# A delta-net layer on one Trainium2 core: v turned by DMA, merges in three pieces, half of an out-projection cut by depth, and a planner with other costs and another order

## The chip, the cores and the metric

The kernel runs on one core of a Trainium2 chip. Its engines are TensorE (PE, with its weight loads shown as PEld), VectorE (DVE), ScalarE (ACT), GpSimd (POOL) and SyncE (SP), whose queue issues nearly all the DMAs of the part in question. The metric is the device time of one execution in microseconds; lower is better. Only the times of the chip count.

## What is computed

A trunk of two layers over a sequence of 1024 rows of 1024 numbers, in float32. Layer 0 is a gated delta-net layer with a convolutional FFN behind it, layer 1 a chunked attention with another FFN. The change lies in the delta-net layer alone, whose reference is, cut to what matters:

```python
proj = xn @ w_in                                   # q, k, v, z and the gates
qkv = silu(causal_dwconv(proj[..., :A_CONV_WIDTH], conv_w))
q, k = l2norm(q) * 128 ** -0.5, l2norm(k)          # 8 heads of 128; v as it is
m = strict_lower(k_beta @ k.T * decay)             # per chunk of 64 rows
u, w = solve(m + eye, [v * beta, k_beta * exp(gcum)])
...
v_new = u_c - w_c @ state                          # chunk after chunk
o_c = qd @ state + a_c @ v_new
state = state * dec + ke.T @ v_new
...
o = rmsnorm(o, out_norm_w) * silu(z)
return o.reshape(bsz, seq, A_V_WIDTH) @ w_out      # + the residual stream
```

## The kernel before, in words

**The dense work.** A product of float32 matrices is done as three matmuls in a reduced format (L118, L119, L120: high part by high part, low by high, high by low), each 128x128 weights against 512 columns. Those three for one depth tile of 128 are called a unit here. A weight tile comes as `wraw` (SP), ACT rounds it to `whi`, and POOL subtracts four pieces to get `wlo` (L101 to L103).

**The delta-net stage.** 24 projection tiles (k, q and v of 8 heads, in the order of the list `ORDER`, L1329), each of two halves of 512 rows (s = 0, 1) and 8 units a half. Behind each half `project` (L601) runs the convolution and silu: `post` on ACT, `taps` on DVE, `silu` on ACT and POOL. A half of v is stored to `d_v` in float32; k and q go on in SBUF or by `d_kq`. Between the units stand the small products of the recurrence: `gram` (L672, `pg`) makes the 128x128 blocks `mn` per head, POOL's copies `cm` of their diagonal blocks go to `d_m`; `invert_blocks` (L785) inverts these on DVE and stores them by ACT's `W` to `d_u`; `merge` (L824), eight times, loads the inverses as `D` from `d_u` (two loads, one for each of its two heads) and joins blocks of 16 to 32, 64 and 128 rows in one PSUM tile `pm`, with copies on ACT (`X`, `TY`, `U`) and DVE (`U`) between its pieces; its last two pieces are eight 64x64 products each (L881 and L886). `prep` (L738) turns k (`pk`, four transposes on PE, scaled by ACT to `ke`), makes `pqk`, and loads a half of v as `vv` from `d_v`, turns it by four PE transposes into PSUM (`pv`, L778) and multiplies it by the scale `sk` on DVE (L780). `chain` and `output` (L912, L897) are the recurrence proper: `pc<-S,kq`, DVE's `vv`, `pc<-vv,U`, ACT's `y`, `pc<-y,ke`, DVE's `S`, and `pu` for the output. `finish` normalizes, `yz` and `split_yt` (L1039, L1056) multiply by the gate and split the result into `xh` (an ACT cast, L1057) and `xl` for the out-projection.

**The out-projection.** `out_tile(m, s)` (L1285): for each of 8 column tiles m of a half s, all 8 depth tiles in one PSUM tile, then one DVE addition of the residual, which a DMA brings as two u16 planes `xm` and POOL and DVE weave into `xs` (L1299). After each tile one step of the FFN's norm follows (`norm_steps`: ACT's square, and ACT's and POOL's `xh`, `xl` with h). All 8 tiles of s = 0 go first, then those of s = 1.

**What sets the order.** `Flow` (L198) is a list planner that runs while the program is built. It keeps a time `wv.T` for PE (0.69 us for a unit, `wv.pe(n, cost)` for small products) and times for ACT, DVE and POOL to which the code books costs (`wv.on("A", 0.8)`). A step goes in when those booked times say that its operands are ready, less a slack. The order of PE, ACT and DVE so made is kept by the compiler; the orders of SP and POOL are set by the framework's scheduler. Nothing of the booked numbers runs on the chip.

Of the kernel before, what the change touches and what calls it, by code (L numbers as in the profile page):

```python
# [16 lines left out]
P = 128  # L17
# [11 lines left out]
def trunk_kernel(  # L29
# [168 lines left out]
    class Flow(Weave):  # L198
# [4 lines left out]
        def __init__(self):  # L203
# [4 lines left out]
            self.brief, self.early, self.split_at, self.hold, self.far = False, 8, 8, None, 4.0  # L208

# [11 lines left out]
        def pe(self, n, dt=0.22):  # L221
            self.T += n * dt

# [46 lines left out]
        def _dense(self):  # L270
# [19 lines left out]
            self.T += 0.69  # L290
# [215 lines left out]
    d_v = [[dram.tile([P, HALF], F32, name=f"d_v{k}_{s}") for s in range(2)] for k in range(KT)]  # L506
    d_kq = [[dram.tile([P, HALF], F32, name=f"d_kq{k}_{j}") for j in range(2)] for k in range(KT)]
    with ExitStack() as ph:
        wp = ph.enter_context(tc.tile_pool(name="wp0", bufs=2, **SB))
        dp = ph.enter_context(tc.tile_pool(name="dp", bufs=1, **SB))  # L510
        tri = dp.tile([P, P], F32, name="tri")
# [12 lines left out]
        ba = dp.tile([P, 8, 16], F32, name="ba")  # L524
# [5 lines left out]
        eg, neg_eg, ekd, dec = gt("eg"), gt("neg_eg"), gt("ekd"), gt("dec")  # L530
        gc = dp.tile([P, 2, 8, 8], F32, name="gc")
        gcum, gtot = gc[:, 0], gc[:, 1]
        gr = dp.tile([64, P], F32, name="gr")
# [15 lines left out]
        ssk, ssq, sk, ck, nck = gt("ssk"), gt("ssq"), gt("sk"), gt("ck"), gt("nck")  # L549
# [3 lines left out]
        tiles = [0, 0]  # L553

# [19 lines left out]
        def split_tile(raw):  # L574
            wt = split_w(raw, [P, KT, P])
            wv.on("G", 2.75, wv.on("A", 1.0))
            return wt
# [23 lines left out]
        def project(m, dsts, key, store=None, n_from=0):  # L601
# [4 lines left out]
            def post(s, ps):  # L606
# [7 lines left out]
                def taps():  # L614
# [6 lines left out]
                    wv.later(wv.on("D", 2.19), silu)  # L621

                def silu():
# [8 lines left out]
                    wv.mark((key[0], key[1], s), t)  # L632

# [16 lines left out]
        def qnorm(hd, s):  # L650
# [5 lines left out]
            wv.pe(4, 0.11)  # L656
# [3 lines left out]
            slot[0] = wv.on("A", 1.9)  # L660
# [11 lines left out]
        def gram(t):  # L672
# [24 lines left out]
            for i, hd in enumerate(hds):  # L697
# [15 lines left out]
                wv.pe(4)  # L713
# [18 lines left out]
                wv.mark(("gram", hd, s), wv.on("G", 1.2, t_) + 2.5)  # L732
# [3 lines left out]
            wv.mark(("scale", t), wv.on("D", 3.5))  # L736

        def prep(hd, s):  # L738
# [12 lines left out]
            wv.pe(4, 0.11)  # L751
# [3 lines left out]
            slot[0] = wv.on("A", 1.4)  # L755
# [4 lines left out]
            vv = dp.tile([P, 4, P], F32, name="vv", tag="vv", bufs=4)  # L760
            nc.sync.dma_start(out=vv.rearrange("p c t -> p (c t)"), in_=d_v[hd][s])
# [6 lines left out]
            wv.pe(4)  # L768
# [4 lines left out]
            t = max(t, wv.on("G", 1.4))  # L773
# [5 lines left out]
            wv.pe(4, 0.11)  # L779
# [1944 lines left out]
```

## Time and profile before

| | |
|---|---|
| median of 3 runs | 2499.27 us (2497.41 to 2501.43) |
| span of the profiled execution | 2493.3 us |
| median less span | 6.0 us |
| PE busy | 2466.1 us, 99% of the span |
| DVE, POOL, ACT busy | 1842.5, 1523.0, 1442.1 us |
| granted TensorE clock | 9 tenths or more in all 40 slices |

The profile gives no time of its own for the profiled execution beside its span; the 6.0 us is what the median of the runs has over that span. A row of the profile gives an engine, a line of the kernel, an operation, "out<-in" by tile names, a shape, a count, and busy time or mean duration. A PE row's duration is longer than the distance to the next row, since matmuls are pipelined; what PE's stream costs is read from the starts. The delta-net stage with its out-projection runs from 21 us to 643 us, where the first matmul of the FFN stands.

### The profile page before, as it was taken

What the parts mean: (1) busy time and instruction counts of PE and PEld (TensorE: products, weight loads), DVE (VectorE), ACT (ScalarE), POOL (GpSimd) and SP (SyncE); (2) the same over time, 40 slices, a digit from 0 to 9 for tenths busy, and PEclk for the clock granted to TensorE, in tenths of its full rate; (3) what the DMA queues carried; (4) which work ended last, traced back from release to release, by engine and by line L of the source; (5) the groups of instructions that cost most, each with busy time, mean ns of one, the idle gap of its engine ahead of it and who ended that gap; (6) DMA issues with size and microseconds to landing.
All of it is one profiled execution on the core that took longest, in us unless ns stands there. A gap on an engine that the chain in (4) does not pass through costs nothing.

```text
span 2493.3 us, 39279 instructions
## 1 busy us (share of the span) xinstructions
PE 2466.1 (99%) x13785; PEld 2057.0 (83%) x13785; DVE 1842.5 (74%) x2985; ACT 1442.1 (58%) x2770; POOL 1523.0 (61%) x1548
## 2 busy tenths in 40 slices
PE   8999999999999999999999999999999999999998
PEld 6888888888888888888788888888877888888877
DVE  5665874567798888888866656666589788888886
ACT  6444546474465556565555666667456565666555
POOL 3655653357357777777626454455554777778774
PEclk9999999999999999999999999999999999999999
DMA  8734435565347777777841232333444799777788
GB/s 228 188 105 118 142 110 153 156 194 163 96 108 148 150 153 151 153 144 156 183 151 55 67 80 77 81 76 95 145 114 119 184 176 180 166 169 171 152 187 224
DMA packets 383877, 353.19 MB, mean 142 GB/s; under 512 B 97600, under 2 KB 304448, under 8 KB 383680
## 3 DMA queue, kind: packets, MB, share of 16 engines
q1 hardware_dynamic: 350704, 243.46, 34.4%
q0 software_dynamic: 28224, 98.58, 22.5%
q10 hardware_dynamic: 4752, 8.65, 0.9%
q8 instruction: 108, 1.77, 0.3%
q14 instruction: 89, 0.73, 0.1%
HBM read 182.25 MB, written 156.30 MB: 136 GB/s over the span
## 4 chain that ended last, share of the span: by engine, by line
PE 81%; POOL 6%; DVE 4%; issue 4%; DMA 2%; ACT 2%; SPq 0%; ACTq 0%; POOLq 0%; DVEq 0%
PE acc L118 8%; PE pu L1448 8%; PE acc L119 8%; PE acc L120 8%; PE pu L1446 8%; PE pu L1447 8%; PE pd L1448 3%; PE pd L1446 3%; PE pd L1447 3%; POOL ul L1412 3%; PE acco L118 2%; PE acco L120 2%; PE acco L119 2%; PE ptp L2353 2%; PE poT L2399 1%
## 5 line engine op out<-in xcount | busy, mean ns | idle before, releaser
L1412 POOL TENSOR_TENSOR ul<-r,uh 128x512 fp32r<-128x512 f32 x266 | 430.4, 1638 | 258.3 <-ACT uh L1434 253.5
L118 PE MATMUL acc<-xh,whi 128*128 128x512 f32 x896 | 369.3, 413 | 0.5 <-ACT xh L1094 0.5
L119 PE MATMUL acc<-xl,whi 128*128 128x512 f32 x896 | 352.1, 393 | 0.4 <-POOL xl L381 0.3
L120 PE MATMUL acc<-xh,wlo 128*128 128x512 f32 x896 | 351.3, 392 | 0.0
L103 POOL TENSOR_TENSOR wlo<-wraw,whi 128x256 fp32r<-128x256 f32 (+1 forms) x326 | 237.0, 758 | 107.8 <-ACT whi L101 105.3
L1434 ACT CAST uh<-r 128x512 fp32r<-128x512 f32 x289 | 177.1, 623 | 183.3 <-DVE r L1412 148.8
L1448 PE MATMUL pu<-xh,ul 128*128 128x512 f32 x524 | 204.4, 390 | 0.7 <-POOL ul L1412 0.7
L1446 PE MATMUL pu<-xh,uh 128*128 128x512 f32 x524 | 204.4, 390 | 0.7 <-ACT keep L1575 0.7
L1802 ACT COPY stage<-pd 128x1024 f32<-128x1024 f32 x180 | 175.3, 1014 | 49.7 <-PE pd L1448 48.8
L1447 PE MATMUL pu<-xl,uh 128*128 128x512 f32 x524 | 203.9, 389 | 0.0
L120 PEld LDWEIGHTS acc<-xh,wlo 128*128 128x128 f32 x896 | 168.5, 188 | 37.1
L2308 POOL TENSOR_SCALAR sS<-sS,st 128x640 f32<-128x640 f32 (+4 forms) x128 | 87.6, 691 | 178.4 <-DVE st L2306 168.2
L119 PEld LDWEIGHTS acc<-xl,whi 128*128 128x128 f32 x896 | 169.3, 189 | 28.4 <-POOL xl L381 2.5
L118 PEld LDWEIGHTS acc<-xh,whi 128*128 128x128 f32 x896 | 169.1, 189 | 27.5 <-ACT xh L1094 0.9
L1412 POOL TENSOR_TENSOR dl<-a,dh 128x512 fp32r<-128x512 f32 x90 | 153.3, 1703 | 47.4 <-ACT dh L1434 37.2
L1541 DVE SCALAR_TENSOR_TENSOR gate<-gpre,colt,gate 128x1023 f32<-128x1023 f32 (+2 forms) x92 | 176.5, 1919 | 2.5 <-ACT gate L1538 1.8
L1541 DVE SCALAR_TENSOR_TENSOR val<-vpre,colt,val 128x1023 f32<-128x1023 f32 x88 | 149.2, 1696 | 29.3 <-ACT val L1538 29.3
L2298 DVE CUSTOM_DVE_ANT_0 sS<-sc,bt 128x640 f32<-128x640 f32 (+4 forms) x128 | 84.1, 657 | 111.4 <-PE sc L2294 75.9
L1412 DVE TENSOR_TENSOR r<-r,r 128x512 f32<-128x512 f32 x160 | 130.3, 814 | 32.8 <-POOL ul L1412 31.7
L1412 DVE TENSOR_TENSOR el<-val,eh 128x512 fp32r<-128x512 f32 x90 | 85.4, 949 | 43.2 <-ACT eh L1434 43.2
L1448 PEld LDWEIGHTS pu<-xh,ul 128*128 128x128 f32 x524 | 98.4, 188 | 22.8 <-POOL ul L1412 1.4
L1446 PEld LDWEIGHTS pu<-xh,uh 128*128 128x128 f32 x524 | 98.4, 188 | 21.1 <-ACT keep L1575 1.1
(428 smaller groups left out, 7197.9 us busy)
## 6 DMA issues: line engine op xcount, KB each, us to landing
r<-in_f_w_up_dram SPq DMA_DIRECT2D x176, 256.0 KB, 4.5
d_r<-stage POOLq DMA_DIRECT2D x78, 512.0 KB, 8.1
d_c<-stage POOLq DMA_DIRECT2D x70, 512.0 KB, 8.4
a<-in_f_w_down_dram SPq DMA_DIRECT2D x72, 256.0 KB, 2.9
wraw<-in_a_w_in_dram SPq DMA_DIRECT2D x32, 512.0 KB, 4.5
d_e<-stage POOLq DMA_DIRECT2D x32, 512.0 KB, 8.3
wraw<-in_a_w_out_dram SPq DMA_DIRECT2D x16, 512.0 KB, 4.1
d_r<-h ACTq DMA_DIRECT2D x32, 256.0 KB, 2.8
```

The costliest lines, as they stand in the source:

```text
L103: nc.gpsimd.tensor_tensor(lo[:, c], raw[:, c], hi[:, c].bitcast(F32), op=ALU.subtract)
L118: mm(ps, hi[:, kw, wcol : wcol + P], rh[k][s], start=st, stop=False)
L119: mm(ps, hi[:, kw, wcol : wcol + P], rl[k][s], start=False, stop=False)
L120: mm(ps, lo[:, kw, wcol : wcol + P], rh[k][s], start=False, stop=sp)
L1412: tt = lambda eng, o, a, b, op: eng.tensor_tensor(o, a, b, op=op)
L1434: copy(hi, src)
L1446: mm(ps, w[0][:, cw], x[0], start=first, stop=False, skip_group_check=True)
L1447: mm(ps, w[0][:, cw], x[1], start=False, stop=False, skip_group_check=True)
L1448: mm(ps, w[1][:, cw], x[0], start=False, stop=last, skip_group_check=True)
L1541: nc.vector.scalar_tensor_tensor(t_[:, a:c1], p_[:, a - step : c1 - step], w[:, 2 - step : 3 - step], t_[:, a:c1], op0=ALU.mult, op1=ALU.add)
L1802: nc.scalar.copy(t_, ps)
L2308: nc.gpsimd.tensor_scalar(S, S, st[:, 3:4], 1.0, op0=ALU.mult, op1=ALU.mult)
```

## The change

Four things are changed in the delta-net layer; the FFNs and the attention are the same but for numbers in names.

1. **v.** After silu an ACT copy `cast` takes v apart into its two u16 halves (`th`), SP stores them to `d_v`, now 1024 rows of 128 u16, and `prep` loads them back by a DMA transpose as `vh`. ACT copies one plane into `vv`, POOL the other, and DVE multiplies by `sk` from SBUF. The four PE transposes `pv` and their PSUM tile go, for 16 halves.
2. **Merges.** The two last pieces of eight 64x64 products become three: four `low`; four pairs of `corner` and `low`; four `corner`. ACT's copies between them are halved in size, four instead of two.
3. **Out-projection, second half.** `out_deep` takes two column tiles at a time and depth tiles 0 to 3 for all 8 column tiles first, then 4 to 7: `h = ps + xs`, then `h = ps + h`. The number of matmuls is the same.
4. **The planner.** Booked costs and slack get other numbers, and `ORDER` is another. Some small tiles share buffers.

The diff, cut to its core:

```diff
-            self.T += 0.69
+            self.T += self.unit + self.mixed
...
-    d_v = [[dram.tile([P, HALF], F32, ...
+    d_v = [[dram.tile([SEQ, P], mybir.dt.uint16, ...
...
+                    if key[0] == "v":
+                        wv.later(t - 0.6, lambda: cast(th))
+                        return
...
+                def cast(th):
+                    nc.scalar.copy(planes(th), woven(d))
+                    nc.sync.dma_start(out=store[s].rearrange("(h b c) t -> c h b t", h=2, b=4), in_=th...)
...
-            vv = dp.tile([P, 4, P], F32, name="vv", tag="vv", bufs=4)
-            nc.sync.dma_start(out=vv.rearrange("p c t -> p (c t)"), in_=d_v[hd][s])
+            vh = dq.tile([P, 2, HALF], U16, name="vh", tag="vh")
+            nc.sync.dma_start(out=vh.rearrange("p h t -> p (h t)"), in_=d_v[hd][s], transpose=True)
...
-            slot = yield from wv.bank()
-            pv = paux.tile([P, HALF], F32, name="pv", tag="pa")
-            for c in range(4):
-                nc.tensor.transpose(pv[:, cs(c)], vv[:, c], ident)
-            wv.pe(4, 0.11)
-            nc.vector.tensor_tensor(vv, pv..., sk..., op=ALU.mult)
+            vv = dp.tile([P, 4, P], F32, name="vv", tag="vv", bufs=4)
+            w_ = woven(vv.rearrange("p c t -> p (c t)"))
+            nc.scalar.copy(w_[:, 0], vh[:, 0])
+            nc.gpsimd.tensor_copy(w_[:, 1], vh[:, 1])
+            yield max(wv.on("A", 0.78), wv.on("G", 0.93)) - wv.slack
+            nc.vector.tensor_tensor(vv, vv, sk..., op=ALU.mult)
...
-            for a, c, n in blocks:
-                mm(pm[64:128, n], mn[a][0:64, c, 64:128], TY[0:64, n], start=True, stop=True)
-            nc.scalar.copy(TY[64:128], pm[64:128])
-            yield wv.on("A", 0.6)
-            for a, c, n in blocks:
-                mm(pm[0:64, n], TY[64:128, n], U[64:128, n, 64:128], start=True, stop=True)
-            nc.scalar.copy(U[0:64, :, 64:128], pm[0:64])
+            for c in range(4):
+                low(0, c)
+            nc.scalar.copy(TY[64:128, 0:4], pm[64:128, 0:4])
+            yield wv.on("A", 0.4)
+            for c in range(4):
+                corner(0, c)
+                low(1, c)
+            nc.scalar.copy(TY[64:128, 4:8], pm[64:128, 4:8])
+            t_ = wv.on("A", 0.4)
+            close(0)
+            yield t_
+            for c in range(4):
+                corner(1, c)
+            close(1)
...
+        def out_deep(ms, k0):
+            raw = wp.tile([P, 4, 2 * P], F32, name="wraw", tag="wraw", bufs=2)
...
+            xms = [out_x(m, 1) for m in ms if k0 == 0]
...
-        ORDER = "k2 k0 k1 k3 q2 q0 q1 k5 k4 q3 v0 v1 k6 v2 v3 k7 q4 q5 q6 q7 v5 v4 v6 v7"
+        ORDER = "k2 k0 q0 q2 q1 k5 k4 k3 k1 k6 v1 v0 k7 q3 v2 v3 q4 q5 v5 v4 q6 q7 v6 v7"
-        wv.slack = 0.5
+        wv.slack = 0.6
+        wv.unit, wv.turnover = 0.683, 0.09
```

Three places show how the order moves. The first is SP's queue at the first merge of the program, before and after. `D` is the merge's load of the inverted blocks, `d_m` gram's store of a later head's blocks, `d_kq` a store of k or q.

```order
L630 DMA d_kq_0_154<-u 128x512
L808 DMA d_u_226<-W 128x512
L571 DMA wraw<-in_a_w_in_dram 128x8x128
L831 DMA D<-d_u_226 128x4x32 x2
L630 DMA d_kq_0_152<-u 128x512
L690 DMA d_e_0_204<-E 128x512
```

```order
L822 DMA d_u_224<-W 128x512
L577 DMA wraw<-in_a_w_in_dram 128x8x128
L845 DMA D<-d_u_224 128x4x32
L639 DMA d_kq_0_158<-u 128x512
L744 DMA d_m_221<-cm 128x4x32
L845 DMA D<-d_u_224 128x4x32
L759 DMA eq<-d_eg 128x4x128
L704 DMA d_e_0_207<-E 128x512
```

The two `D` loads stood together; now the second stands behind a `d_kq` and a `d_m` store.

The second is ACT's queue at the last merge, before and after. `X`, `TY` are the merge's copies, `ke` is of `prep`, `xh` are the casts of out-projection operands, `y` is of the chain.

```order
L865 COPY X<-pm 32x256 x2
L868 COPY TY<-T 32x8x32 x2
L1057 CAST xh_0_6133<-spare 128x512
L906 COPY vv<-pu 128x128
L876 COPY TY<-pm 32x8x32
L935 ACTIVATE y<-pc,ck 128x128 x2
L906 COPY vv<-pu 128x128
L883 COPY TY<-pm 64x512
```

```order
L879 COPY X<-pm 32x256 x2
L882 COPY TY<-T 32x8x32 x2
L768 ACTIVATE ke<-pk,ekd 128x128 x4
L1086 CAST xh_0_6294<-spare 128x512
L1086 CAST xh_0_6296<-spare 128x512
L1086 CAST xh_0_6298<-spare 128x512
L1086 CAST xh_0_6300<-spare 128x512
L1086 CAST xh_0_6302<-spare 128x512
L1086 CAST xh_0_6304<-spare 128x512
L964 ACTIVATE y<-pc,ck 128x128
L890 COPY TY<-pm 32x8x32
L935 COPY vv<-pu 128x128
```

One cast stood between the merge's first `TY` copies and its next; now six casts and four `ke` stand there.

The third is POOL's queue in the second half of the out-projection, at its first weight tiles; `xl` with `h` is of the FFN's norm.

```order
L1299 COPY xs<-xm 128x512
L103 TENSOR_TENSOR wlo<-wraw,whi 128x256 x4
L1299 COPY xs<-xm 128x512
L381 TENSOR_TENSOR xl_0_7200<-h_1_6584,xh_0_7199 128x512
L103 TENSOR_TENSOR wlo<-wraw,whi 128x256 x4
L1299 COPY xs<-xm 128x512
L381 TENSOR_TENSOR xl_0_7204<-h_3_6586,xh_0_7203 128x512
L103 TENSOR_TENSOR wlo<-wraw,whi 128x256 x4
```

```order
L103 TENSOR_TENSOR wlo<-wraw,whi 128x256 x4
L1328 COPY xs<-xm 128x512 x2
L103 TENSOR_TENSOR wlo<-wraw,whi 128x256 x4
L1328 COPY xs<-xm 128x512
L384 TENSOR_TENSOR xl_0_7225<-h_1_6599,xh_0_7224 128x512
L1328 COPY xs<-xm 128x512
L384 TENSOR_TENSOR xl_0_7229<-h_3_6601,xh_0_7228 128x512
L103 TENSOR_TENSOR wlo<-wraw,whi 128x256 x4
L1328 COPY xs<-xm 128x512 x2
L384 TENSOR_TENSOR xl_0_7233<-h_5_6603,xh_0_7232 128x512
```

A weight tile's `wlo` had one `xs` beside it; in the first depth half it has two.

## Rows read from the trace of the kernel before

**Rows 1.** The page's head, the program's one execution:

```profile
span 2493.3 us, 39279 instructions
```

**Rows 2.** Windows: length; PE, PEld, DVE, ACT, POOL busy; clock, DMA, GB/s:

```profile
21.00:643.00 622.00, 621.57 (x5019) 522.00 (x5018) 394.00 (x1013) 327.65 (x876) 340.69 (x448) 1.00 0.53 151
```

**Rows 3.** Timeline of PE, 172 to 174 us (start, us, line, tile, shape):

```profile
172.56 0.39 PE L120 MATMUL acc<-xh,wlo 128*128 128x512 f32 x1
172.78 0.60 PE L778 MATMUL pv<-ident,vv 128*128 128x128 f32 x4
...
173.69 0.40 PE L120 MATMUL acc<-xh,wlo 128*128 128x512 f32 x1
```

**Rows 4.** Timeline of PE, a 64x64 merge piece (two records a product):

```profile
187.87 0.38 PE L939 MATMUL pc<-y,ke 128*128 128x128 f32 x2
188.19 1.14 PE L881 MATMUL pm<-TY,mn 64*64 64x64 f32 x16
189.26 0.49 PE L903 MATMUL pu<-S,kq 128*128 128x128 f32 x2
```

**Rows 5.** Timeline of PE, a merge piece of 32x32 tiles:

```profile
152.28 0.75 PE L845 MATMUL pm<-T,mn 32*32 32x32 f32 x64
```

**Rows 6.** DMA issues: operation, count, KB each, median us from issue to landing:

```profile
D<-d_u SPq DMA_DIRECT2D x16, 64.0 KB, 3.3
```

**Rows 7.** One tile of the attention layer, vt (ns: least, median, most):

```profile
L2229 ACT COPY vt<-acc x14: 1012/1012/1012, 1377.3 to 1717.6; 128x1024 uint16<-128x1024 uint16 x14
```

**Rows 8.** One tile of the attention layer, vu, loaded by DMA transpose:

```profile
L2212 ACT COPY vf<-vu x28: 755/779/796, 1391.7 to 1740.2; 128x512 uint16<-128x512 uint16 x28
L2206 SPq DMA_TRANSPOSE vu<-d_vt x14: 1160/1171/2198, 1380.9 to 1730.7; - x14
```

**Rows 9.** One tile, xs, a half's worth of u16:

```profile
L1299 POOL COPY xs<-xm x16: 758/926/1242, 541.1 to 634.5; 128x512 uint16<-128x512 uint16 x16
```

**Rows 10.** One line, L1280, the input's DMA transposes at 11 to 73 us:

```profile
L1280 SPq DMA_TRANSPOSE xm<-in_x_dram x16: 1159/1258/6186, 11.4 to 72.6; - x16
...
DMA to landing us min/median/max: 3.1/3.8/7.8
```

**Rows 11.** Lines of ACT, 100 to 560 us (count, busy, mean ns, idle before):

```profile
L101 ACT CAST whi<-wraw 128x1024 fp32r<-128x1024 f32 x29 | 30.3, 1044 | 0.0
...
L689 ACT ACTIVATE E<-E,ngc 128x128 f32<-128x128 f32 x51 | 16.2, 391 | 0.3 <-DVE E L686 0.2
...
L610 ACT ACTIVATE u<-acc,colt 128x509 f32<-128x509 f32 x18 | 12.4, 686 | 29.7 <-PE acc L120 24.8 <-POOL u L627 2.6 <-issue 2.3
...
L806 ACT ACTIVATE W<-B,even 128x256 f32<-128x256 f32 x4 | 2.0, 506 | 2.8 <-DVE B L803 2.8
```

**Rows 12.** Lines of POOL, the same stretch:

```profile
L627 POOL TENSOR_TENSOR u<-u,th 128x512 f32<-128x512 f32 x27 | 35.2, 1305 | 2.2
L626 POOL TENSOR_SCALAR th<-th 128x512 f32<-128x512 f32 x38 | 24.5, 644 | 70.1 <-ACT th L625 50.9 <-DVE B L803 4.9 <-DVE u L616 4.8
...
L729 POOL COPY cm<-mn 32x128 f32<-32x128 f32 x52 | 16.7, 322 | 24.5 <-DVE mn L724 22.6
```

**Rows 13.** Lines of DVE, the same stretch:

```profile
L841 DVE STREAM_TRANSPOSE T<-D 128x256 f32<-128x256 f32 x8 | 3.5, 436 | 4.4 <-DMA D<-d_u 4.4
```

**Rows 14.** Timeline of ACT, 514 to 533 us:

```profile
515.02 2.18 ACT L1057 CAST xh<-spare 128x512 fp32r<-128x512 f32 x4
...
529.54 1.14 ACT L754 ACTIVATE ke<-pk,ekd 128x128 f32<-128x128 f32 x4
...
531.21 0.74 ACT L865 COPY X<-pm 32x256 f32<-32x256 f32 x2
```

**Rows 15.** Waits, 21 to 643 us (total us, times, longest):

```profile
DVE U L878 <- ACT TY L876: 12.6, 6, 3.8
```

**Rows 16.** Timeline of POOL, 607 to 624 us:

```profile
608.85 2.84 POOL L103 TENSOR_TENSOR wlo<-wraw,whi 128x256 fp32r<-128x256 f32 x4
...
613.37 1.30 POOL L381 TENSOR_TENSOR xl<-h,xh 128x512 fp32r<-128x512 f32 x1 [0.74 <-ACT xh L393]
```

More of the change, by code (lines that the diff above doesn't have):

```diff
@@ L1299, in out_tile, with out_end @@
                 (nc.gpsimd, nc.vector)[i].tensor_copy(hm[:, :, i], xm[:, i])
-            wv.on("G", 0.60), wv.on("D", 0.6)
-            for k in range(KT):
-                dense(ps, wt, 0, *acts, FULL[k : k + 1], s, first=k == 0, last=k == KT - 1)
-                if k < KT - 1:
-                    yield
+            wv.on("G", 0.95), wv.on("D", 0.69)
+            return ps, xs
+        def out_end(m, s, ps, xs):
             nc.vector.tensor_tensor(h[m][:, hs(s)], ps, xs, op=ALU.add)
@@ L1319, in then, with out_unit, out_tile @@
                         wv.add(1.2, "normed", lambda: t0 + 0.54, tail(its[s]))
-            wv.later(wv.on("D", 0.64), then)
-            yield
+            wv.later(wv.on("D", 0.69), then)
+        def out_unit(ps, wt, s, k):
+            dense(ps, wt, 0, *acts, FULL[k : k + 1], s, first=k == 0, last=k == KT - 1)
+        def out_tile(m, s):
+            raw, xm = out_raw(m, s)
+            yield
+            wt = split_tile(raw)
+            yield 4
+            ps, xs = out_begin(xm)
+            for k in range(KT):
+                out_unit(ps, wt, s, k)
+                if k < KT - 1:
+                    yield
+            out_end(m, s, ps, xs)
+            yield
+        def out_deep(ms, k0):
+            raw = wp.tile([P, 4, 2 * P], F32, name="wraw", tag="wraw", bufs=2)
+            nc.sync.dma_start(out=raw, in_=a_w_out[k0 * P : (k0 + 4) * P, ms[0] * P : (ms[1] + 1) * P].rearrange("(k p) m -> p k m", p=P))
+            xms = [out_x(m, 1) for m in ms if k0 == 0]
+            yield
+            wt = split_w(raw, [P, 4, 2 * P])
+            wv.on("G", 2.9, wv.on("A", 1.04))
+            yield 4
+            for n, m in enumerate(ms):
+                if k0 == 0:
+                    ps, xs = out_begin(xms[n])
+                else:
+                    ps, xs = pacc.tile([P, HALF], F32, name="acco", tag="acc", bufs=3), h[m][:, hs(1)]
+                for k in range(4):
+                    dense(ps, wt, n * P, *acts, [(k, k0 + k)], 1, first=k == 0, last=k == 3)
+                    if k < 3:
+                        yield
+                if k0 == 0:
+                    nc.vector.tensor_tensor(h[m][:, hs(1)], ps, xs, op=ALU.add)
+                    wv.on("D", 0.69)
+                else:
+                    out_end(m, 1, ps, xs)
+                yield
         def tail(it):
@@ L1377, in trunk_kernel @@
                 wv.add(3, ("gate", k % 2), wv.when(("z", k, 1), *[("act", e, 0) for e in range(8)]), gate(k, 1))
[L1378 to L1380 removed]
+            for m in range(KT):
+                wv.dense.append((lambda: True, there("begun", *[("act", k, 0) for k in range(KT)]), out_tile(m, 0)))
+            for k0 in (0, 4):
+                for m in range(0, KT, 2):
+                    wv.dense.append((lambda: True, there(*[("act", k, 1) for k in range(k0, k0 + 4)]), out_deep((m, m + 1), k0)))
             wv.run(lambda: not (wv.dense or wv.items or wv.late or wv.cur or wv.nxt))
```

129 lines of the change are left out of this document (69 added, 60 removed).

## The prediction, made before the changed kernel was run

> **What bounds the kernel.** The head of the page gives the span, 2493.3 us [rows 1]; the median of the runs is 6.0 us above it, and I carry that difference over. The change lies in the stretch from 21 to 643 us, so the next view is the table of windows for that stretch alone: PE is busy 621.57 of 622.00 us at a granted clock of 1.00, while DVE, ACT and POOL are busy for 394, 328 and 341 us [rows 2]. So PE's stream, put end to end, is the time of this stage. The sum therefore has two kinds of terms: what PE no longer issues (a sure gain), and new waits of PE on work that used to come in time. The other engines have room on the mean (53 to 63% busy), so added work there counts only where it stands ahead of something that PE waits for. The timeline of PE gives the price of each kind of product from the distance between starts, not from the listed durations, which overlap.
>
> **PE's work, part by part.**
> *The transposes of v.* One `pv` group stands in the dense stream between the start of one L120 at 172.56 and that of the L120 of the next unit at 173.69: 1.13 us [rows 3]. A unit alone takes 0.69 us (the planner's number, which three matmuls at the later distances of 0.23 confirm). The group costs 0.44 us, and 16 groups go: -7.0 us.
> *The merges.* A piece of eight 64x64 products, sixteen records, starts at 188.19 and the next product at 189.26, 1.07 us later; the two records ahead of it, of 0.11 each, leave 0.10 for going in [rows 4]. Of the 1.07, the products take 0.94 (0.117 each) if leaving costs 0.13. Three pieces in place of two add one going in and out: 0.10 to 0.23, I take 0.19, eight times: +1.5. But the middle piece alternates `corner` and `low`, which use different quarters of the array. Rows of the same kernel show that products on different parts do run side by side: 64 records of 32x32 take 0.75 us [rows 5], 0.012 each, against 0.059 for a 64x64 record. If each pair takes the time of one, four products of 0.117 are saved per merge; I take 0.38 of these 0.47, eight times: -3.0. Together -1.5, with +1.5 as the bound without overlap and -3 where the extra going in is free.
> *The dense stream.* Units, out-projection products and the rest keep their number. By the changed order the stream is broken by small products 14 times more than before, eight of which are the third pieces; the other six at some 0.07: +0.4.
> Work of PE: -7.0 - 1.5 + 0.4 = **-8.1 us**, between -5.1 and -10.
>
> **What v by DMA adds beside PE.** The attention layer does the same with its v, so each new operation has an equal there. A half costs ACT 1.01 us for taking the planes apart [rows 7] and 0.78 for one plane back [rows 8], 16 times: 29 us on top of 328 in 622. POOL gets 0.93 a half [rows 9], 15 us on top of 341. SP is held 1.17 us by a transpose [rows 8]; it lands after 3.8 us [rows 10]. DVE's product is the same, from SBUF rather than PSUM. All this is hidden as long as POOL and ACT are not late for something else; I cost it at nothing by itself, and at most by what rival two says. `prep` asks for v some 5 us before it is used, which covers 3.8.
>
> **New waits of PE.** What the new order does to the queues is seen in three places shown above.
> *First merge.* The second `D` load now stands on SP behind the store of blocks of a later head (`d_m`), which can't go before gram's copies `cm`. The chain from the end of that head's projection: on ACT convolution 0.69, `cast` 1.01, four `E` 1.56, four `ke` 1.14, two `W` 1.0, `whi` 1.04 [rows 7, 11, 14] = 6.4; on POOL four `wlo` 2.84, two `th` 1.29, two products 2.61, four `cm` 1.29 [rows 12, 16] = 8.0; then SP's issue, about 0.4, the load 3.3 [rows 6], DVE's `T` 0.44 [rows 13]. The sum is 18.6; some 15 instructions in a row start 0.05 to 0.1 before the last one's listed end, which leaves 17.6. PE has meanwhile 17 units (11.6), four transposes and twelve 128x128 products (3.1): 14.8. Wait **+2.8**, bounds 0 (ACT's and POOL's steps not all in this row) and 4.
> *Last merge.* On ACT four `ke` and six casts now stand between the merge's first `TY` copies and its next one, where one cast stood. Four casts take 2.18 [rows 14], six 3.2. DVE's `U` copies wait for that `TY` copy already now [rows 15], and the chain's `vv` on DVE stands behind them, and `pc<-vv,U` on PE behind that. The chain: `X` 0.74, `ke` 1.14 [rows 14], casts 3.2, and seven short ones (`y`, three `TY`, two `U`, `vv`) at the 0.37 of one `X`: 7.7. PE has in that time five units, five products of 0.22, four transposes and 24 small ones: some 6.0. Wait **+1.7**, bounds 0 and 3.7.
> *Out-projection, first depth half.* A weight tile of four depths by two columns has eight units, 5.5 us. POOL has to give it `wlo` 2.84, two `xs` 1.85 and an `xl` 1.30 [rows 9, 16]: 6.0, and before it was 5.1, so POOL falls back by 0.5 or more at each of four tiles. The weights are two tiles ahead, which covers the first. Wait **+1.4** over tiles three and four, bounds 0 and 4. In the second depth half `xs` goes, and POOL is ahead again.
> Other waits in this order come to nothing that I can show: solve, chain and gate have their old distances.
> Waits: 2.8 + 1.7 + 1.4 = **+5.9 us**, between 0 and 11.7.
>
> **The sum.** -8.1 + 5.9 = -2.2. The profiled span would go from 2493.3 to 2491.1, the median from 2499.3 to **2497.1**. The planner's new numbers act through the order alone and have no term beside the waits. FFNs and attention begin 2 us earlier with the same order; nothing in them looks at the clock of this stage.
>
> **A rule against this change.** Each merge goes into and out of another tile shape once more; the rows show 0.10 us for going in and about 0.13 for going out [rows 4]. The Trainium skill, TensorEngine Tiling (Array Packing), section Key Properties, says that changing the tiling mode drains TensorE. By that rule, read at its hardest, rival four below would be the result; the trace shows less at the place read, so the sum keeps 0.19.
>
> **The rivals.** Measurements of this kernel differ by some 0.2% (5 us) before a difference can be told from none.
> *One: the slack covers the waits.* The three chains were added from listed means; if each is 3 us shorter, or if POOL's and SP's orders turn out kinder when run, no wait remains, and PE's -8.1 is the result: **2491.2**. For it: the stage before has next to no wait, though its means give chains almost as tight. Against: the `d_m` store ahead of the `D` load is in the queue, and can't be passed. Chance 0.28.
> *Two: the transposes of v come late, and it is slower.* When the DMA engines are loaded, the same kind of transpose held SP up to 6.2 us and landed after up to 7.8 [rows 10]. In this stage they share SP with weight loads, `d_m` and `D`; POOL's plane copy stands in order ahead of `wlo` and `cm`, so a late plane holds both. It decides where the landing's median goes past about 6 us: past the 5 us of `prep` and POOL's slack of about 1. At 7.8 each lacks about 2; if eight of 16 pass 2.2 us on to PE, +17.6: -2.2 + 17.6 = +15.4, **2514.7**. Against: outside that stretch their maximum on SP is 2.2 us [rows 8], and the stage moves 151 GB/s. Chance 0.12.
> *Three: the pairs don't run side by side.* The change then does not do what it says for the merges; PE's work is -5.1, the waits stay, the sum is +0.8: **2500.1**. Against: 32x32 products do overlap [rows 5]. Chance 0.15.
> *Four: a change of tile shape costs PE a whole matmul each way* where the third pieces stand. At the 0.39 us that a matmul is listed with [rows 3], eight more pieces cost 6.2 in place of 1.5; the sum is +2.5: **2501.8**. Against: the 0.10 and 0.13 read above. Chance 0.05.
> My forecast has the remaining 0.40.
>
> **Range and chances.** The forecast's own bounds, waits 0 to 11.7 and PE -5.1 to -10, are not all met at once; 2490 takes in rival one, and 2507 the forecast with every wait at its upper bound (+3.6, 2502.9) and the mildest third of rival two. Outside lie most of rival two and little else: 0.2. Faster by over 5 us needs waits under 3.1: rival one and a small part of the forecast, 0.33. Slower by over 5 us: rival two and a few cases of the forecast with another late chain, 0.14. Same: 0.53.
>
> **What would show it.** PE of 21 to 640 us should have some 8 us less of work, and waits of PE on `T` or DVE's `D` step at the first merge (about 2.8), on DVE's `vv` or ACT's `TY` near the last merge (1.7), and on `wlo` in the out-projection (1.4). A `low`/`corner` piece of 16 records should take about 0.7 us; 1.07 would be rival three. The landing of `vh` should be under 5 us. If PE waits nowhere, rival one holds; if it waits on `wlo` or `vv` again and again through the stage, rival two. The forecast is wrong if waits add up to under 3 or over 11 us, or if the FFNs' spans differ.

## The result, and the profile after

The changed kernel takes 2505.79 us (median of 8 runs, 2504.09 to 2511.66), the kernel before 2498.76 us (8 runs beside them, 2496.65 to 2501.43). The medians differ by 7.0 us; the ratio is 1.0033, interval 1.0023 to 1.0043. (Ratios leave disturbed runs out, so they are not always the quotient of the medians.) It is slower. The forecast was 2497.1, no change; 2505.79 lies in its range of 2490 to 2507, but the kernel was forecast 2 us quicker and came out 7 us slower; that it would be slower by over 5 us had a chance of 0.14.

The profiled execution's own time is 2507.46, 1.7 above its span of 2505.8. A second trace of the kernel before has 1.8 there (span 2495.6, time 2497.36), so the 6.0 us that the prediction carried over were no fixed cost: the first trace of before [rows 1] was a quick execution.

The change ends where the first FFN begins. Timeline of PE, the FFN's first matmul, in the changed kernel:

```profile
652.07 0.39 PE L1516 MATMUL pu<-xh,uh 128*128 128x512 f32 x1
```

and in the kernel before:

```profile
643.24 0.39 PE L1446 MATMUL pu<-xh,uh 128*128 128x512 f32 x1
```

The stage is 8.8 us longer (7.4 against the second trace of before, where it began at 644.7). From there to the last matmul it is 1843.3 and 1844.1 us in the two traces of before and 1846.5 in the changed one. That part had between 1843.9 and 1856 in the traces of the experiments, with the same code, so its 2 us are not laid to the change. (About 1846 had been expected of the second trace of before; it stayed at 1844.1.)

The window that answers to [rows 2], for the changed kernel (same columns):

```profile
21.00:652.00 631.00, 619.38 (x4957) 514.14 (x4956) 410.75 (x1023) 356.16 (x924) 357.32 (x465) 0.99 0.57 149
```

PE was busy for all but 0.4 us of its 622 before; now 11.6 us are idle, and the clock is no longer 1.00. Who was waited for, in the list of waits of PE, 21 to 652 us (total us, times, longest):

```profile
PE pm L859 <- DVE T L855: 3.8, 1, 3.8
PE pc L959 <- DVE vv L957: 3.3, 4, 1.9
PE acco L120 <- POOL wlo L103: 1.9, 3, 1.6
PE pm L865 <- issue: 1.2, 2, 0.7
PE pc L959 <- DVE vv L794: 0.7, 1, 0.7
PE pq L669 <- POOL kq L633: 0.5, 1, 0.5
PE pc L955 <- DVE S L974: 0.2, 1, 0.2
```

The first three are the three places of the prediction. Before, the same list had two waits of 0.2.

**The clock.** Windows of the changed kernel around its two longest pauses (length; PE, PEld, DVE, ACT, POOL busy; granted clock, DMA share, GB/s):

```profile
193.00:197.00 4.00, 0.20 (x20) 0.16 (x22) 2.23 (x6) 1.95 (x5) 2.42 (x4) 1.00 0.41 97
197.00:198.00 1.00, 1.00 (x66) 0.85 (x59) 0.96 (x2) 0.24 (x1) 0.00 (x0) 0.89 0.20 53
198.00:201.00 3.00, 3.00 (x66) 2.06 (x68) 2.79 (x15) 0.77 (x2) 0.00 (x0) 0.50 0.93 155
201.00:202.00 1.00, 1.00 (x25) 0.76 (x17) 1.00 (x5) 0.00 (x0) 0.00 (x0) 0.91 0.95 222
...
536.00:539.00 3.00, 3.00 (x11) 2.61 (x11) 1.04 (x2) 0.92 (x2) 1.28 (x1) 0.50 0.86 317
```

PE stands still from 193 to 197; when it works again the clock is full for most of the first microsecond, then 0.50 (1.2 instead of 2.4 GHz) for three. The time lost is the missing clock times the length: 0.11 + 1.5 + 0.09 = 1.7 us after the first pause. After the second, which ends at 534.23, it is 1.5 in the three us shown and 0.2 in the windows beside them (0.92 over two us, 0.95 over one), 1.7 again. At these two places a pause costs 1.7 us more than its own length: 3.8 + 1.7, and 1.9 + 1.7.

**The account of the stage.** Listed waits +11.2 (11.6 less the 0.4 of before). A wait is listed from the listed end of the product ahead, which lies about 0.16 us behind the point where the next could have started (0.39 long, starts 0.23 apart [rows 3]); 13 waits: +2.1. The clock: +3.4. That is +16.7; with the stage at +8.8, PE's own work is 7.9 us less. This is what the other terms leave over and no reading of its own. Counted in another way, by the excess of every distance between starts over the median of its kind in the kernel before, it is 8.3 less. The forecast for this term was 8.1.

### The profile page after: what moved, and what is told of

It is laid out like the page before. It is cut to its first block, busy times and chain, and to the rows that moved or that the text cites. A ratio compares the mean times of both kernels' runs of the same rounds, so it can differ in the third digit from the quotient of the medians.

```text
span 2505.8 us, 39175 instructions
## 1 busy us (share of the span) xinstructions
PE 2465.2 (98%) x13721; PEld 2049.1 (82%) x13721; DVE 1859.4 (74%) x2993; ACT 1470.1 (59%) x2818; POOL 1539.3 (61%) x1564
## 4 chain that ended last, share of the span: by engine, by line
PE 74%; POOL 7%; DVE 6%; issue 6%; DMA 3%; ACT 3%; SPq 0%; POOLq 0%; ACTq 0%; DVEq 0%
PE pu L1518 7%; PE acc L118 7%; PE acc L119 7%; PE acc L120 7%; PE pu L1516 7%; PE pu L1517 7%; PE pd L1516 3%; PE pd L1518 3%; PE pd L1517 3%; POOL ul L1482 3%; PE ptp L2423 2%; PE acco L118 2%; PE acco L120 2%; PE acco L119 2%; PE poT L2469 1%
```

## The experiments

The theory is that the time is lost in the queues: the new order puts steps of SP, ACT, POOL and DVE behind others, so that what PE needs comes late at a few places; and where PE stops for long, the clock adds to it. The rivals named with the runs put the loss on one added operation, or on one of the three parts for itself. All ratios are against the kernel before on the same chip; its medians were 2497.9 to 2500.2.

**One load of D.** The first merge's wait, from the other side: SP's queue in the changed kernel, 188 to 195 us.

```profile
188.72 0.53 SPq L845 DMA_DIRECT2D D<-d_u  x1
...
193.60 0.36 SPq L744 DMA_DIRECT2D d_m<-cm  x1
194.01 0.50 SPq L845 DMA_DIRECT2D D<-d_u  x1
```

As read from the order, the second `D` stands behind `d_m`, and `d_m` goes when the last `cm` has been copied. Then the load, DVE's `T`, and PE:

```profile
196.34 0.45 DVE L855 STREAM_TRANSPOSE T<-D 128x256 f32<-128x256 f32 x1 [1.67 <-DMA D<-d_u]
```

```profile
196.84 0.75 PE L859 MATMUL pm<-T,mn 32*32 32x32 f32 x64 [3.79 <-DVE T L855]
```

(The next two matmuls start at 197.52 and 197.92, 0.40 apart and not 0.23: the clock.) What holds `cm`, and so `d_m`, back goes over ACT and the new `cast` of v:

```profile
180.34 1.05 ACT L644 COPY th<-u 128x1024 uint16<-128x1024 uint16 x1 [1.28 <-POOL u L633]
...
184.27 1.04 ACT L101 CAST whi<-wraw 128x1024 fp32r<-128x1024 f32 x1
```

From `cast` to the end of `whi` ACT has no pause; POOL's `wlo` starts at 185.39, right behind `whi`, and from there POOL has no pause up to the end of `cm` at 193.58. The experiment takes the load out of its place behind `d_m`:

```diff
-            for a in range(2):
-                nc.sync.dma_start(out=D[:, 4*a:4*a+4], in_=d_us[t][2*j+a].rearrange("c b j i -> (b j) c i"))
+            nc.sync.dma_start(out=D, in_=d_us[t][2*j:2*j+2].rearrange("a c b j i -> (b j) (a c) i"))
```

> The changed kernel with one edit: a merge's two loads D become one load for both heads, so the load of the first merge no longer stands behind the store of a later head's blocks. Nothing moves on PE, ACT, DVE and POOL. Theory Q (PE's work fell by 8 us as forecast; the loss is a few waits that the order of the queues makes, and each of the two long ones is followed by about 3.2 us at half clock): the wait of 3.8 us at 197 us goes, but the next thing behind it, the load of v's second half, holds POOL's copy of a plane and behind it a product for kq, so PE waits some 3 us for kq at about 204 us instead. Time about the same as the changed kernel, 2504 to 2507. Rival L (the one late load is the whole cause at this place): the wait and the clock's fall go, 3.8 + 1.6 us less, 2500.4.

2507.81 us, ratio 1.0038 [1.0024, 1.0053], just above the 2504 to 2507 expected: nothing gained. Of its waits of PE:

```profile
PE pq L669 <- POOL kq L633: 3.3, 2, 3.0
...
PE pm L858 <- DVE T L854: 2.1, 1, 2.1
```

The wait on `T` falls by 1.7, not to nothing, and one on `kq`, 7 us later, rises by 2.8. Why `kq` is late stands in POOL's timeline of this kernel:

```profile
202.24 0.75 POOL L792 COPY vv<-vh 128x512 uint16<-128x512 uint16 x1 [6.40 <-DMA vh<-d_v]
```

POOL stood for 6.4 us at its plane copy, waiting for a transpose of v that SP had issued at 195.72, and `kq`, the next in its queue (202.93, 1.26 long), stood behind it. In the changed kernel PE came later to this place and hardly noticed. The wait had moved to the next late thing, and the half clock with it: behind the pause of 2.1 us the clock is 1.00 (196 to 203 us), behind that of 3.0 us it is 0.50 (204 to 207).

**And the plane copy off POOL.** The second plane then goes to DVE:

```diff
-            nc.gpsimd.tensor_copy(w_[:, 1], vh[:, 1])
+            nc.vector.tensor_copy(w_[:, 1], vh[:, 1])
```

> The same one load, and the copy of v's second plane moved from POOL to DVE, right ahead of the product that reads both; no other engine's order changes. Theory Q: POOL is no longer held by a late transpose, so neither the wait at 197 us nor one for kq stays, nor the half clock behind it; together 3.8 + 1.6 + 0.7 and some of the small waits: about 2499, 6 to 7 us below the changed kernel. The wait before the last merge (1.9 us, clock down after it) and those for wlo stay. Rival T (the transposes' lateness itself, 6.0 us median, is the cause, wherever its copies stand): chain products wait for DVE's vv instead, and the time stays above 2503.

2502.63 us, ratio 1.0013 [1.0004, 1.0022]. About 2499 was expected. The wait on `kq` is 0.7, as forecast, but that on `T` is 2.5: by medians 3.2 us are gained of the 6 to 7. DVE's timeline of this kernel shows why `T` is late although `D` is there:

```profile
191.29 1.29 DVE L700 TENSOR_TENSOR E<-E,negm 128x512 f32<-128x512 f32 x1
192.51 0.54 DVE L792 COPY vv<-vh 128x512 uint16<-128x512 uint16 x1
192.94 2.31 DVE L626 SCALAR_TENSOR_TENSOR kq<-acc,colt,kq 128x512 f32<-128x512 f32 x3
195.16 0.43 DVE L854 STREAM_TRANSPOSE T<-D 128x256 f32<-128x256 f32 x1
```

`T` has no idle time ahead of it: it is DVE's own queue now, `E`, the three convolution steps and the plane copy that this edit puts there. In the changed kernel DVE's queue was done at 194.67 and stood 1.67 us for the load, which hid its own lateness. PE's wait on v's product (`vv` L794) rises from 0.7 to 1.6, the sign of rival T, but not by its cause: the transposes still land after a median of 6.0 us, and yet all that waits for one in this trace is DVE, once, for 0.6; ahead of the late product DVE's queue, with the new copy in it, has no pause.

**POOL relieved in the out-projection.** The three waits on `wlo` were forecast to come from POOL's queue. One weight tile of the changed kernel:

```profile
614.95 3.30 POOL L103 TENSOR_TENSOR wlo<-wraw,whi 128x256 fp32r<-128x256 f32 x4 [3.00 <-ACT whi L101]
...
619.13 1.84 POOL L384 TENSOR_TENSOR xl<-h,xh 128x512 fp32r<-128x512 f32 x1
...
621.84 1.28 POOL L384 TENSOR_TENSOR xl<-h,xh 128x512 fp32r<-128x512 f32 x1
623.08 3.50 POOL L103 TENSOR_TENSOR wlo<-wraw,whi 128x256 fp32r<-128x256 f32 x4
```

Two `xs` of 1.0 stand where lines are left out. From `wlo` to `wlo` it is 8.1 us, against 6.0 by the prediction, which had one `xl` in a tile and each step at its undisturbed length; PE's eight units take 5.5. But the first row also shows that POOL had stood idle for 3.0 us ahead of this tile until ACT had rounded `whi`, so POOL's queue is not the whole of it. The edit gives ACT the `xs` of every second column tile (`n == 1`):

```diff
-                (nc.gpsimd, nc.vector)[i].tensor_copy(hm[:, :, i], xm[:, i])
+                if i == 0 and act:
+                    nc.scalar.copy(hm[:, :, i], xm[:, i])
+                else:
+                    (nc.gpsimd, nc.vector)[i].tensor_copy(hm[:, :, i], xm[:, i])
```

> The changed kernel with one edit: of the two xs of a weight tile in the first depth half of the out-projection, one has its first plane woven by ACT instead of POOL (four copies). Theory Q: PE's waits for wlo at 624 to 632 us (2.1 us with what follows them) go, nothing else moves: 2503.7. Rival W (wlo is late for another reason, the weights' load or ACT's rounding): no change, 2505.8.

2504.45 us, ratio 1.0018 [1.0010, 1.0027]; the wait on `wlo` falls from 1.9 to 0.9. By medians 1.3 us less where 2.1 was expected, and the intervals overlap. The direction is that of POOL's queue; with half of the wait left, and POOL idle for `whi` ahead of it, rival W (ACT's rounding) keeps a share that no run separates.

**No depth cut.** The out-projection as it was before, the rest as changed: `out_deep` and its helpers replaced by the old loop over tiles of all eight depths.

```diff
-            for k0 in (0, 4):
-                for m in range(0, KT, 2):
-                    wv.dense.append((..., out_deep((m, m + 1), k0)))
+            for s in range(2):
+                for m in range(KT):
+                    wv.dense.append((..., out_tile(m, s)))
```

> The changed kernel with the out-projection's second half as in the kernel before (whole depth, column tile by column tile); all else as changed. Theory Q: the cut by depth gives PE nothing and costs waits for wlo, which go: 2.1 us less, 2503.7. Rival D (the cut lets the second half start before its late operands are there): PE waits for xh or xl of depth tiles 4 to 7 at the second half's start, and the time is 2506 or more.

2503.49 us, ratio 1.0017 [1.0008, 1.0026], where 2503.7 was expected, and a wait on `wlo` of 0.2. The cut by depth cost about 2.3 us by medians (4 by the ratios, whose intervals overlap a little); the list gives 1.7, and the overhangs add some 0.3.

**The edits together.** The two of the first merge, `xs` on ACT, and the six casts of the last merge at least 0.7 us apart in the plan. The last merge in the changed kernel, ACT's timeline:

```profile
529.03 3.23 ACT L1086 CAST xh<-spare 128x512 fp32r<-128x512 f32 x6
...
532.55 0.36 ACT L890 COPY TY<-pm 32x256 f32<-32x256 f32 x1
```

then DVE, and PE:

```profile
532.95 0.85 DVE L892 COPY U<-pm 32x256 f32<-32x256 f32 x2 [4.46 <-ACT TY L890]
533.83 0.35 DVE L957 SCALAR_TENSOR_TENSOR vv<-pc,neg_eg,vv 128x128 f32<-128x128 f32 x1
```

```profile
534.23 0.49 PE L959 MATMUL pc<-vv,U 128*128 128x128 f32 x2 [1.88 <-DVE vv L957]
```

It is the chain of the prediction's second wait, step by step, and 1.88 us against 1.7. The edit beside the three shown:

```diff
+        spaced = [0.0]
...
+            while wv.T < spaced[0]:
+                yield spaced[0]
+            spaced[0] = wv.T + 0.7
```

> The three edits of the runs sent with this one, and a fourth: the casts of out-projection operands are let in at least 0.7 us of planned time apart, so that six of them no longer stand in a row ahead of the last merge's copy. Theory Q: the four places with waits are gone but for about 1.2 us in two short waits near 540 us, and the clock stays at full speed; the PE work of the changed kernel stays 8 us below that of before. About 2492.5, between 2490 and 2495, faster than before by 6 us. Rival T: not under 2499, since v's late transposes find another wait.

2501.12 us, ratio 1.0003 [0.9994, 1.0012]: by the ratio all of the loss is back, and the expectation of 2492.5 was still missed by 8.6. The long wait on `vv` is gone (four of 0.4 at most remain) and `wlo` is 0.6; `T` is 2.5, another `vv`, v's product, 1.6. The sum of the listed waits up to the FFN at 646.9 is 7.0. The clock, expected to stay up, is 0.51 from 196 to 199.5 us, behind the pause on `T`: another 1.7. The time is rival T's (not under 2499) without its cause: the wait on v's product is the one seen with the two edits, behind DVE's own queue.

**The pause filled.** To see the clock by itself, PE is given 15 products that nothing reads (an addition to the computation, without effect on the output) in the pause ahead of the first merge:

```diff
+            if (t, j) == (0, 0):
+                for r in range(15):
+                    mm(pm[:, 0:2].rearrange("p c i -> p (c i)"), ident, ident, start=True, stop=True)
```

> The changed kernel with 15 idle products of 128x128 (about 3.4 us, into a PSUM tile that is written anew right after) ahead of the first merge's piece, where PE waits 3.8 us at 197 us; nothing is taken from the wait's cause. It computes the same. Theory Q (the clock falls because PE paused): PE is busy up to about 196.5 us, the clock stays at full speed in 197 to 201 us, and the stage is 1.6 us shorter though nothing comes earlier: 2504.2. Rival R (the clock falls for what comes behind, or at that time of the program, whatever PE did): half clock at 198 to 201 us as before, 2505.8 or more.

The stretch of three us that ran at 0.50 in the changed kernel, here:

```profile
198.00:201.00 3.00, 3.00 (x77) 2.33 (x76) 2.79 (x15) 0.63 (x1) 0.00 (x0) 1.00 0.91 157
```

and the merge's products behind the filler:

```profile
192.70 3.51 PE L859 MATMUL pm<-ident 128*128 128x128 f32 x30
196.70 0.75 PE L862 MATMUL pm<-T,mn 32*32 32x32 f32 x64 [0.49 <-DVE T L855]
```

With PE busy over the pause the clock stays at 1.00, and the products of this stretch stand 0.23 apart. So the half clock comes from the pause. 2504.2 was expected; the total is 2506.99, ratio 1.0031 [1.0019, 1.0043], and no gain shows in it. At 205 us PE waits 1.9 for `kq` (0.5 in the changed kernel), which takes back what the clock gave. The clock's 1.7 us is thus shown in the trace and not in the total. The stage does end 2.8 us earlier (649.30), but by two things that the edit does not touch: the clock stays at 1.00 behind the last merge's pause too (533 to 541 us), and the stalls inside a piece (1.2 us) are missing. The total of the profiled execution, 2513.98, is no measure of the edit: its part behind the stage, with the same code, takes 1856 us.

**The parts alone.** Three runs cut the change another way. First v by DMA alone, put into the kernel before with its old numbers and list (the diff is the part on `d_v`, `cast`, `vh` and `vv` that stands above):

> The kernel before with v by DMA alone (stores of planes, DMA transposes, plane copies, no transposes on PE), the merges, the out-projection, the planner's numbers and the list of tiles as before. Theory Q (order decides): PE's work falls by 7 us, but the planner books the new steps beside old numbers and lays the last two merges and chains so tight that some 18 us of waits come, most of them between 515 and 555 us on ACT's and DVE's part of the chains, with several falls of the clock behind the longer ones: 2511 to 2518. Rival P (the part is worth its 7 us where it is done alone, and the changed planner is what loses): about 2493.

2521.34 us, ratio 1.0099 [1.0077, 1.0121], above the 2511 to 2518 expected. PE's listed waits add up to 15.8, and the clock is near 0.50 over 400 to 404, 530 to 540, 547 to 554, 561 to 564 and 609 to 612 us, which takes about 13 more. Then all three parts, v, merges and out-projection, with the old numbers and list:

> The kernel before with v by DMA, the three-piece merges and the out-projection cut by depth together, with the old booked numbers and the old list of tiles. Theory Q: PE's work is 8 us less, waits of about 25 us, clock falls of 1.6 us behind each longer one: 2516 to 2526; that is, the planner's new numbers and list in the change are what takes 10 to 20 us of waits away again. Rival P: 2491 to 2493.

2531.36 us, ratio 1.0127 [1.0111, 1.0142], where 2516 to 2526 was expected. And the numbers, slack and list alone, in the kernel before:

```diff
-        wv.slack = 0.5
+        wv.slack = 0.6
+        wv.unit, wv.turnover = 0.683, 0.09
...
-            wv.pe(32, 0.03)
+            wv.pe(32, 0.022)
...
```

> The kernel before with the planner's new numbers, slack and list of tiles alone; every step of the program as before. Theory Q: PE's work is the same, and waits of about 2 us come (at a load of v near 515 us, at wlo near 624 us), 2501 to 2504, with no gain: the new numbers are worth nothing where nothing needs them. Rival P (numbers that are nearer to the measured times make a better order by themselves): 2496 or less.

2510.14 us, ratio 1.0045 [1.0030, 1.0060], where 2501 to 2504 was expected. None of the three is good alone, and they are not terms of a sum (by medians): parts in the old plan +33, plan without parts +12, both +7. So what an order is worth hangs on the parts in it. All three runs were slower than expected: the direction was right, the size too small. In the second of these, PE waits 4.8 us on `U`, 3.3 on `vv` of the output, 3.2 on `y`, 3.1 on `X`, 2.7 on `S`: everywhere a little.

**The changed kernel without v by DMA.** If v by DMA is what loses, its removal should win. The diff is that part reversed, and the rest stays as changed.

> The changed kernel without its first part: v is stored in float32 and turned by PE again, as in the kernel before; merges in three pieces, the out-projection cut by depth, the planner's new numbers and list stay. Theory Q (the new list and numbers are built around v by DMA, which is worth its PE work there): PE has 7 us more to do, some waits at the first merge and one before the out-projection stay, 2507 to 2511, that is slower than the changed kernel by 2 us or more. Rival V (v by DMA is what loses, by its late transposes and by POOL's and DVE's extra work): 2502 or less.

2514.64 us, ratio 1.0057 [1.0043, 1.0072], above the 2507 to 2511 expected. The rival falls as a cause of the whole loss: with the new list, v by DMA is worth 6 us by the ratios (8.8 by medians). That this is near the 7.0 of PE's work says little, since this kernel has other waits (13.7 us in the list, the changed kernel 11.6) and loses more to the clock (5.1 us, the changed kernel 3.4). Its two longest waits of PE:

```profile
PE pv L781 <- DMA vv<-d_v: 5.9, 1, 5.9
PE acco L120 <- POOL wlo L103: 4.9, 4, 3.2
```

PE does not wait on `T` at all here. ACT has no `cast` ahead of the first merge, and its timeline has `whi` earlier:

```profile
181.56 1.03 ACT L101 CAST whi<-wraw 128x1024 fp32r<-128x1024 f32 x1
```

That is 2.7 us before the changed kernel's, and `d_m` goes at 191.59 instead of 193.60, which is about half of the 3.8; the planner also lays the merge later for PE. So the first wait is probably in part the doing of v by DMA; the order differs too, so this is not shown by itself.

**Another list.** If the order is the cause, another one could keep the 8 us: one load, the planes on ACT and DVE, spaced casts, no depth cut, slack 0.5, and

```diff
-  "k2 k0 q0 q2 q1 k5 k4 k3 k1 k6 v1 v0 k7 q3 v2 v3 q4 q5 v5 v4 q6 q7 v6 v7"
+  "k2 k0 q0 q2 q1 k4 k3 k5 k1 v1 k6 v0 k7 q3 v2 q4 v3 v4 v5 q6 q5 q7 v6 v7"
```

> The changed kernel with one load of D, both planes of v copied by ACT and DVE, the casts 0.7 us apart, the out-projection as in the kernel before (no cut by depth), the slack 0.5 again, and another list of tiles (k2 k0 q0 q2 q1 k4 k3 k5 k1 v1 k6 v0 k7 q3 v2 q4 v3 v4 v5 q6 q5 q7 v6 v7), picked so that the chains, with durations as the changed kernels' traces have them, leave no wait over about 1.1 us. Theory Q: PE's 8 us come out but for some 4 us of short waits, no fall of the clock: 2494 to 2496, faster than before by 3 to 5 us. Rival T: new waits of over 1.5 us with falls of the clock in other places, 2499 or more.

2500.56 us, ratio 1.0004 [0.9995, 1.0012]: no change against before, 4 to 6 above what was expected. It is the time of rival T, and its signs are there: waits of 2.6, 1.9 and 1.6, and the clock at 0.50 from 196 to 199 and from 544 to 547 us. Its largest wait is in no plan. PE's timeline of this kernel:

```profile
192.96 0.74 PE L864 MATMUL pm<-D,X 32*32 32x32 f32 x62
196.26 0.26 PE L864 MATMUL pm<-D,X 32*32 32x32 f32 x2 [2.57 <-issue]
```

PE stops with 62 of 64 records of like products done, which read the same two tiles, for 2.6 us. This execution took 2505.55, 5 us above the median of its kernel, so what the stall costs in the median isn't known. The same stall, shorter, stands in the changed kernel's list above (`pm L865 <- issue`, 1.2), in the second trace of before (1.2), and in the planner alone (2.3). It is missing in the first trace of before. Its cause stays open.

## Why the prediction was wrong

**PE's work: right.** Forecast 8.1 us less; 7.9 and 8.3 by the two counts above. The parts hold too. A `corner` and `low` piece of sixteen records, in PE's timeline of the changed kernel, begins, and the next product behind it:

```profile
216.26 0.27 PE L898 MATMUL pm<-U,TY 64*64 64x64 f32 x1
...
216.88 0.50 PE L118 MATMUL acc<-xh,whi 128*128 128x512 f32 x1
```

Sixteen records in 0.62 us, where sixteen of one kind took 1.07 [rows 4]: the pairs run side by side, and rival three falls. A piece of eight records begins at 214.07, and the next product at 214.67:

```profile
214.07 0.68 PE L895 MATMUL pm<-TY,mn 64*64 64x64 f32 x8
214.67 0.50 PE L118 MATMUL acc<-xh,whi 128*128 128x512 f32 x1
```

That is 0.60, so a third piece costs no whole matmul each way, and rival four falls. The Trainium skill, TensorEngine Tiling (Array Packing), section Key Properties, has the change of mode drain TensorE; these rows leave 0.13 us for it in a piece of four products (0.60 less four of the prediction's 0.117), against the 0.19 that the prediction took.

**The waits: the step that failed.** "Waits: 2.8 + 1.7 + 1.4 = +5.9" has the three places right, the first two with their mechanism and the third with a part of it, and is too small in three ways. Listed waits of 11.6 also pass the 11 that the prediction gave as a sign of its being wrong.

- *The places themselves*: 3.8, 1.9 and 1.9, 7.6 in place of 5.9. The bound of 4 on the first was close. Its chain took 18.5 us (from 178.37, the convolution on ACT, to 196.84) instead of 17.6: ACT stood 1.3 us for POOL's product ahead of `cast`, which the chain does not have, the load was 1.1 quicker than its 3.3, and the other 0.7 is spread over the steps. At the third, POOL's steps were longer than the undisturbed means that went into the sum (8.1 us a tile, not 6.0).
- *"Other waits in this order come to nothing that I can show"*: there were eight more, 4.0 us in the list (three on `vv` of the same line, 1.4; the stalls inside a piece, 1.2; `vv`, `kq` and `S`, 1.4), and the overhang of 13 waits, 2.1, was in no term.
- *No term for the clock.* A pause was priced at its length; the two longest cost 1.7 us each on top, 3.4 in all. [Rows 2] show a stage at 1.00 that had no pause, so no row of it could say what one would do. The Trainium skill, TensorE: Matmul & The Clock Gate, section HAM oscillation — how this bites in real kernels, says that gaps between bursts of matmuls bring TensorE back to its lower clock; the fall after the pause of 3.8 us agrees, and after those of 1.9 us the runs show one at some times and none at others (below).

Together 5.9 became 16.7 (7.6 + 4.0 - 0.4 + 2.1 + 3.4), and the -2.2 of the stage became +8.8.

**"All this is hidden": half right.** v by DMA lands later than the forecast. Of the tile `vh` of the changed kernel (ns: least, median, most; then who waited, us and times; then landing):

```profile
L775 SPq DMA_TRANSPOSE vh<-d_v x16: 1159/1210/3587, 180.5 to 523.7; - x16
...
  POOL vv L792: 50.1, 10
...
DMA to landing us min/median/max: 3.1/6.0/8.2
```

6.0 us and not 3.8 [rows 10], which is the point from which rival two was to decide. POOL did wait for it, 50.1 us in ten places, with the next steps of its queue behind it, and yet in the changed kernel only 0.5 us of PE's waits are on a product of POOL behind such a copy: POOL has the room. That changes when another wait goes, as the one load showed (3.0 us on `kq`). So rival two's mechanism exists, at a thirtieth of its price; the loss of 7 us is not its 17.6.

**"DVE's product is the same, from SBUF rather than PSUM": wrong.** Lines of DVE in the changed kernel, 21 to 652 us (count, busy, mean ns, idle before):

```profile
L700 DVE TENSOR_TENSOR E<-E,negm 128x512 f32<-128x512 f32 x16 | 15.1, 943 | 4.6 <-DMA E<-d_g 4.6
L794 DVE TENSOR_TENSOR vv<-vv,sk 128x512 f32<-128x512 f32 x16 | 13.9, 866 | 1.8 <-ACT vv L791 1.8
L783 DVE TENSOR_TENSOR at<-pqk,at 128x512 f32<-128x512 f32 x16 | 11.0, 688 | 11.0 <-PE pqk L781 11.0
```

The product with `sk` took 684 ns from PSUM before; with both operands in SBUF it takes 866 in the mean, though 680 where POOL does nothing beside it. `E`, whose operands were in SBUF before too, went from 737 to 943, while `at`, which reads PSUM, stayed at 688 (689 before). Timelines of DVE and of POOL of the changed kernel show what it waits for:

```profile
190.56 0.68 DVE L783 TENSOR_TENSOR at<-pqk,at 128x512 f32<-128x512 f32 x1
191.16 1.28 DVE L700 TENSOR_TENSOR E<-E,negm 128x512 f32<-128x512 f32 x1
```

```profile
190.60 1.29 POOL L633 TENSOR_TENSOR u<-u,th 128x512 f32<-128x512 f32 x1
```

`at` runs beside POOL's product at its usual length; `E` begins in its middle and ends 0.55 us after POOL's end at 191.89; alone it takes 0.68, so it stood for most of what was left of POOL's product. The Trainium skill, SBUF — State Buffer, section Who interferes with whom, states it: VectorE and GpSimd share a pair of ports under an exclusive lock, and a VectorE instruction with two SBUF inputs contends with a GpSimd instruction that reads SBUF. These rows agree. By line it is 16 times 0.18 and 16 times 0.21 us, 6.2 us of DVE's time. One case reaches PE: the product with `sk` at 336.13 takes 1.26 us beside `wlo`, and PE waits 0.7 for it. The long `E` above stands in the queue ahead of the late `T`, where the load hid it.

**What stays open.** Why PE stalls inside a piece of like products. How the third wait divides between POOL's queue and ACT's rounding. Whether a list exists that keeps the 8 us: the two versions tried came to before's time, and none beat both kernels.

## What to carry to other kernels

In a stage whose bound engine never waits, removed work is the sure term and the small one: the gain of 8 us was met, and the waits of the new order, with overhang and clock, took back 17. Price a wait with the overhang and the clock that follow it, and follow each queue to the next late step, since taking one wait away showed the next (`D`, then `kq`, then DVE's own queue). An operand that moves from PSUM to SBUF is a change of its own on DVE, to be looked up in rows where POOL works beside it.

## What the runs showed of the hardware that was not expected

- A like pause is not always followed by the half clock. The wait on `vv` at the last merge was 1.9 us in the changed kernel and in the one without the depth cut; the clock after it was 0.50 for three us in the first, and in the second the mean of 533 to 541 us was 1.00 (its pause ended at 534.86). With the plane copy on DVE and with the filled pause it was 1.00 too, with `xs` on ACT and with the one load 0.79, all after a wait of 1.9. Behind the first merge's 3.8 us it was 0.50 for three us in the changed kernel and for six (196 to 202 us) in the one without the depth cut. What decides was not found.
- Stalls of 0.5 to 2.6 us inside a run of like 32x32 products (64 records, in the kernel before 32), in eight of the fourteen traces, among them one of the two of the kernel before.
- In the run with the other list one `vh` transpose held SP for 4.09 us, where the median of the changed kernel is 1.21. It ran from 192.66 to 196.75, over the whole of PE's stall of 2.6 us; beside the two stalls of the changed kernel (near 231 and 440 us) there is no transpose.
